# A hybrid decoder block on one core: three weight tiles rounded into other rooms, 512-column products in the compressed branch, one gate for both attention groups, keys copied out by ACT

## The chip, the cores and the metric

The kernel runs on one core of one Trainium2 chip. The metric is the device time of one execution in microseconds (us). The time before is the median of three runs. Profiles and traces come from one execution recorded by the hardware profiler, whose own time is told beside its span.

## The reference

One decoder layer over 512 tokens of width 1024, all in float32. The input is normalised, projected by `w_in`, and goes through two mixers whose results are gated and merged:

```python
h = rms_norm(x, norm_pre)
proj = h @ w_in
(q_n, k_c, v_c, k_s, v_s, k_w, v_w, g_n, z_n,
 q_r, k_r, v_r, z_r, m_a, m_b) = jnp.split(proj, split_points(), axis=-1)
...
def compress_blocks(kv, pe, w1, w2):
    ...
    flat = blocks.transpose(0, 2, 1, 3).reshape(n_cmp, G, CMP_LEN * dh)
    return jax.nn.gelu(flat @ w1) @ w2
...
y_a = (o_a * jax.nn.silu(z_n)) @ w_nsa_o
...
q_r = apply_rotary(q_r.reshape(B, S, RET_HEADS, RET_QK_DIM), ret_ang)
k_r = apply_rotary(k_r.reshape(B, S, RET_HEADS, RET_QK_DIM), ret_ang) * (RET_QK_DIM ** -0.5)
o_b = jax.vmap(retention_sequence)(q_r, k_r, v_r.reshape(B, S, RET_HEADS, RET_V_DIM))
y_b = (o_b * jax.nn.silu(z_r)) @ w_ret_o
merged = jax.nn.sigmoid(m_a) * y_a + jax.nn.sigmoid(m_b) * y_b
x = x + rms_norm(merged @ w_out, norm_post)
```

Mixer A is sparse attention with 8 heads of 64 in two key/value groups and three branches (compressed, selected, sliding). In the compressed branch 32 tokens of keys or values are flattened and go through a small network: `flat @ w1` has 2048 inputs and 256 hidden units, once for keys and once for values. Mixer B is retention with 4 heads in chunks of 128 tokens.

## The kernel before

**Split products.** Every float32 operand of a matmul is kept as a rounded high part and a low part (the remainder, rounded). A product is three matmuls: high by high, high by low and low by high. A weight tile of 128x512 therefore goes three ways. A load brings 128x1024 from memory into `raw` (4 slots, issued on SP, L373). ACT (L200) or DVE (L208) copies half of it rounded into `whi`. DVE subtracts (L212, `wlo<-raw,whi`); this is called a split below. The pairs `whi`, `wlo` are rings of NW = 9 places; a place is free again when the last product with its tile is done. A raw slot is free when both its halves are split. The 8 weight tiles of block C (280 columns) have rooms of their own (`WC`). The tiles are numbered by the order in which PE uses them; tiles 24 to 39 are those of the compressed branch.

**Stages of PE.** The main row of the program, in order: A (x by the first weights, 4 tiles at once), C (280 columns of small projections, 4 token tiles t), Q (the attention queries, t from 3 down to 0), the hidden layer of the compressed branch for keys and for values (`hidden(0)`, `hidden(1)`), Z, MA, ZR, then the retention queries and keys, values and state, MB, the output products of both mixers, and the last product. Z and the later blocks have 512 columns. The attention itself (scores, softmax, products with values, in units of a token tile t and a group g) is interleaved behind Q. Some products are done by sums of quarters, whose operands (`hs`, `wmT`, `wqT`) are added up on DVE or by POOL's DMAs, written to memory and loaded again.

**What sets the order.** A static list scheduler (`Order`) writes all instructions while the program is built. It models the clocks of the engines; each piece of work is a generator that yields the time or the event it needs, and the scheduler issues the piece with the best priority that its model holds ready. Each engine then runs its rows in exactly this order. The weight rounding has the priority `rank(p)`: 0 (first) when its tile is due within a window of the model's time, 4 otherwise; for the tiles 24 to 39 the window is 4000 ns. A change of a cost or a condition can thus move rows on every engine.

**What the change touches.** `PHL` is a ring of three rooms of 1024 columns for attention's probabilities, split into both parts, and `PC` is one room for the compressed branch; all lie in `arena_r`. `qT[t]` holds the split and transposed queries. `hidden(i)` multiplies the flattened blocks `Xs[i]`: per weight tile and half of it two matmuls of 256 columns, moving `whi` and `wlo`, summed in the same PSUM half. `compress` goes on with that sum. `att_sum` gathers one unit (t, g), gates it (DVE, `szn`), and writes the result over the gate. `tail_qk` without `base` takes the keys of retention out of PSUM with their row scale `rs` and applies the rotary tables in four `SCALAR_TENSOR_TENSOR` operations of 256 columns per token tile. `ga_split` splits the gated attention for the output product. PSUM banks come from the rings ACC, PS, PT and PO with two banks each.

## Time and profile before

| | us |
|---|---|
| median of 3 runs | 511.99 (511.87 to 512.14) |
| profiled execution | 512.8 |
| its span | 511.0 |
| mean granted TensorE clock | 0.996 |

The profile names groups of instructions by line, engine, operation and tile: `L233 PE MATMUL bank<-whi,hTh` is a matmul of line 233 that writes a PSUM bank from the tiles whi and hTh. PE is TensorE's matmul, PEld its weight load, DVE VectorE, ACT ScalarE, POOL GpSimd, SP the engine that issues DMAs. In timeline rows the first number is the start in us from the span's start, the second the length of the row (several alike instructions may be one row, with their count), and the bracket holds the idle time before it and what ended it. In rows of groups the numbers behind the bar are busy us in all, mean ns of one, and idle us before them. The ends of matmuls are modelled and overlap the next start, so paces are read from starts.

### The profile page before, as it was taken

Reading aid. Unit: us, or ns where it says so; the run is one execution under the profiler, and the core shown is the slowest. Engines: PE = TensorE matmul, PEld = TensorE weight load, DVE = VectorE, ACT = ScalarE, POOL = GpSimd, SP = SyncE. Lnnn points to the kernel's source line nnn. Section 1 sums busy time; section 2 is a strip of 40 time slices with the busy share of each in tenths; the row PEclk is TensorE's granted clock in tenths of the full one; section 3 lists DMA queues with packets and bytes.
Section 4 is the critical chain, followed back from the end, with each engine's and each line's share of the span. In section 5 each row is a group of like instructions: output and inputs, shape, how many; then the busy total and the mean of one; then the engine's idle time right before and its main releaser. Section 6 shows DMA issues by size and latency. Waiting matters only on the chain.

```text
span 511.0 us, 7894 instructions
## 1 busy us (share of the span) xinstructions
PE 501.7 (98%) x2700; PEld 429.6 (84%) x2700; DVE 424.4 (83%) x984; ACT 312.7 (61%) x675; POOL 50.2 (10%) x82
## 2 busy tenths in 40 slices
PE   8999999999999999999999999999999999999994
PEld 7898789888888888888888878888888999888884
DVE  6799699979979799898689899785757769969887
ACT  5788589755777769755585667554614445427541
POOL 2100100002000000101212010311010000000011
PEclk9999999999999999999999999999999999999998
DMA  8996667967921733958389989376875996314826
GB/s 309 378 337 216 177 150 227 345 144 160 252 41 50 223 60 107 325 126 226 79 249 290 315 270 304 61 208 123 279 177 152 322 387 249 123 41 147 275 50 148
DMA packets 34248, 103.47 MB, mean 202 GB/s; under 512 B 3600, under 2 KB 8080, under 8 KB 34192
## 3 DMA queue, kind: packets, MB, share of 16 engines
q1 hardware_dynamic: 29312, 85.41, 47.1%
q0 software_dynamic: 4752, 17.30, 20.0%
q8 instruction: 21, 0.34, 0.3%
q10 hardware_dynamic: 144, 0.26, 0.2%
q14 instruction: 19, 0.16, 0.1%
HBM read 98.76 MB, written 34.08 MB: 260 GB/s over the span
## 4 chain that ended last, share of the span: by engine, by line
PE 80%; DVE 11%; DMA 7%; issue 1%; ACT 1%; SPq 0%; DVEq 0%; ACTq 0%
PE bank L233 74%; DMA raw<-in_stream_dram 7%; PE bank L237 6%; DVE wlo L212 3%; DVE arena_f L212 3%; DVE arena_r L212 2%; DVE nat L212 1%; DVE arena_f L225 1%; DVE arena_f L688 0%; ACT whi L200 0%; ACT arena_r L200 0%; SPq L605 0%; DVE whi L208 0%; DVE st L1362 0%; DVE hTl L225 0%
## 5 line engine op out<-in xcount | busy, mean ns | idle before, releaser
L212 DVE TENSOR_TENSOR wlo<-raw,whi 128x512 fp32r<-128x512 f32 x196 | 127.7, 685 | 9.1 <-ACT whi L200 8.5
L200 ACT ACTIVATE whi<-raw 128x512 fp32r<-128x512 f32 x175 | 103.1, 624 | 46.4 <-PE bank L233 23.3
L233 PE MATMUL bank<-whi,hTh 128*128 128x512 f32 x248 | 96.1, 403 | 0.0
L233 PE MATMUL bank<-whi,hTl 128*128 128x512 f32 x248 | 93.3, 392 | 0.3 <-DVE hTl L225 0.3
L233 PE MATMUL bank<-wlo,hTh 128*128 128x512 f32 x248 | 93.0, 391 | 0.0
L233 PE MATMUL bank<-arena_r 128*128 128x256 f32 (+2 forms) x328 | 69.3, 337 | 0.0
L233 PE MATMUL bank<-hTh,whi 128*128 128x512 f32 (+1 forms) x192 | 66.2, 345 | 0.0
L233 PE MATMUL bank<-arena_r,whi 128*128 128x512 f32 (+1 forms) x224 | 64.9, 374 | 0.0
L233 PE MATMUL bank<-hTh,wlo 128*128 128x512 f32 (+1 forms) x192 | 64.8, 338 | 0.0
L233 PE MATMUL bank<-hTl,whi 128*128 128x512 f32 (+1 forms) x192 | 64.7, 337 | 0.0
L200 ACT ACTIVATE arena_r<-bank 128x512 fp32r<-128x512 f32 (+2 forms) x76 | 42.5, 569 | 30.7 <-PE bank L237 28.3
L233 PEld LDWEIGHTS bank<-whi,hTl 128*128 128x128 f32 x248 | 46.4, 188 | 11.2 <-DVE hTl L225 1.0
L233 PEld LDWEIGHTS bank<-arena_r 128*128 128x128 f32 x328 | 50.3, 189 | 5.7
L233 PEld LDWEIGHTS bank<-whi,hTh 128*128 128x128 f32 x248 | 46.6, 188 | 8.7 <-ACT hTh L200 0.2
L233 PEld LDWEIGHTS bank<-wlo,hTh 128*128 128x128 f32 x248 | 46.7, 188 | 8.4
L212 DVE TENSOR_TENSOR arena_r<-bank,arena_r 128x512 fp32r<-128x512 f32 (+2 forms) x68 | 43.9, 654 | 11.2 <-ACT arena_r L200 10.8
L200 ACT ACTIVATE arena_f<-arena_f,stat 128x128 f32<-128x128 f32 (+3 forms) x88 | 47.5, 552 | 7.2 <-DVE stat L212 4.1
L233 PEld LDWEIGHTS bank<-arena_r,whi 128*128 128x128 f32 x224 | 41.0, 188 | 7.4
L233 PE MATMUL bank<-whi,arena_r 128*128 128x512 f32 (+1 forms) x152 | 44.5, 359 | 0.0
L233 PE MATMUL bank<-arena_r,wlo 128*128 128x512 f32 (+1 forms) x112 | 41.9, 374 | 0.0
L233 PEld LDWEIGHTS bank<-hTh,wlo 128*128 128x128 f32 x192 | 36.4, 190 | 4.1
L233 PEld LDWEIGHTS bank<-hTh,whi 128*128 128x128 f32 x192 | 36.5, 190 | 3.0
(160 smaller groups left out, 773.2 us busy)
## 6 DMA issues: line engine op xcount, KB each, us to landing
raw<-in_stream_dram SPq DMA_DIRECT2D x73, 512.0 KB, 4.8
arena_f<-in_xT_dram SPq DMA_DIRECT2D x16, 256.0 KB, 6.0
wqT<-in_stream_dram POOLq DMA_DIRECT2D x8, 512.0 KB, 5.5
wmT<-in_stream_dram POOLq DMA_DIRECT2D x8, 512.0 KB, 8.0
raw<-wqT SPq DMA_DIRECT2D x8, 512.0 KB, 5.3
woT<-in_stream_dram POOLq DMA_DIRECT2D x8, 512.0 KB, 5.6
raw<-wmT SPq DMA_DIRECT2D x8, 512.0 KB, 5.1
raw<-woT SPq DMA_DIRECT2D x8, 512.0 KB, 3.4
```

The costliest lines, as they stand in the source:

```text
L200: S.activation(o, i, func, **kw)
L212: (V if e == "dve" else G).tensor_tensor(o, a, b, op=op)
L225: V.scalar_tensor_tensor(o, a, s, b, op0=op0, op1=op1)
L233: T.matmul(ps, a, b, start=start, stop=stop)
L237: T.transpose(ps, a, idn)
```

## The change

Four things are changed, and the scheduler's order with them.

1. The tiles 25, 26 and 27 (the second to fourth of `hidden(0)`) no longer take a place of the ring. They have rooms in `arena_r` that stand empty until later: those of `PHL` and `PC` (tiles 25 and 26) and that of `qT[0]` (tile 27). `PHL` begins with one room and `PC` with none; both get theirs when tile 26 is used, and `qT[0]` waits for tile 27 (flag "away"). The window of `rank` becomes 4500 for tiles 24 to 31 and the common one for 32 to 39.
2. `whi` and `wlo` become one tile `whl` with both parts side by side. `hidden` issues one matmul of 512 columns (256 of the high part, 256 of the low) instead of two of 256, so the two sums stand in two halves of a bank, and `compress` adds them.
3. The gate of the attention is applied once per token tile for both groups (`att_gate`, 128 partitions) instead of once per group (64 partitions). `ga_split` waits for it by flags of its own.
4. `tail_qk` without `base` has ACT copy the keys with their scale from PSUM; the rotary tables are then applied from this copy, with two multiplications of 256 columns and one of 512.

```diff
@@ -267,8 +267,8 @@
     Xs = [at(44 + 8 * i, 2048, FR).rearrange("p (l s c) -> p l s c", l=16, s=2) for i in range(2)]
-    PHL = Ring([at(o, 1024, FR) for o in (60, 64, 40)])
-    PC = Ring([at(68, 512, FR)])
+    PHL = Ring([at(o, 1024, FR) for o in (40,)])
+    PC = Ring([])
     qk = [at(44 + 4 * t, 1024, FR).rearrange("p (s c) -> p s c", s=2) for t in range(NT)]
@@ -355,9 +355,11 @@
+    away = {25: 62, 26: 66, 27: 0}
+
     def in_ring(p):
-        return min(p, KD) + max(p - 2 * KD, 0)
+        return min(p, KD) + max(p - 2 * KD, 0) - sum(q < p for q in away)
     hook = {}
@@ -388,7 +390,7 @@
                 p = 2 * i + k
-                own = KD <= p < 2 * KD
+                own = KD <= p < 2 * KD or p in away
                 yield lambda: own or in_ring(p) < in_ring(len(done)) + NW
@@ -398,16 +400,23 @@
                 src = raws[i][0][:, k * m:(k + 1) * m]
-                if own:
+                if p in away:
+                    both = at(away[p], 1024, FR).rearrange("p (s c) -> p s c", s=2)
+                    hi, lo = both[:, 0, :], both[:, 1, :]
+                    pairs_of[p] = both
+                elif own:
                     hi, lo = WC[p - KD]
                 else:
-                    hi = wp.tile([P, 512], FR, name="whi", tag="whi", bufs=NW)
-                    lo = wp.tile([P, 512], FR, name="wlo", tag="wlo", bufs=NW)
+                    both = wp.tile([P, 2, 512], FR, name="whl", tag="whl", bufs=NW)
+                    hi, lo = both[:, 0, :], both[:, 1, :]
+                    pairs_of[p] = both
                 vh, vl = hi[:, :m], lo[:, :m]
...
                 yield
+
+    pairs_of = {}
@@ -528,7 +537,7 @@
             b = now_in[0]
-            return 0 if b is None or b.until(p) <= (4000.0 if 24 <= p < 40 else SOON) else 4
+            return 0 if b is None or b.until(p) <= (4500.0 if 24 <= p < 32 else SOON) else 4
         return fn
@@ -805,13 +814,23 @@
             yield blk.ready(c)
-            hi, lo, r = blk.views(c)
+            r = blk.views(c)[2]
             for l in range(2):
                 st = Xs[i][:, 2 * c + l].rearrange("p s c -> p (s c)")
-                mm(ph[:, 0:256], st, hi[:, l * 256:(l + 1) * 256], c + l == 0, False, r)
-                e = mm(ph[:, 0:256], st, lo[:, l * 256:(l + 1) * 256], False, c + l == 8)
+                e = mm(ph, st, pairs_of[blk.base + c][:, :, l * 256:(l + 1) * 256], c + l == 0, c + l == 8, r,
+                       0.4418 * 512 + 1)
                 yield
             used_up(e)
+            p = blk.base + c
+            if p in away:
+                if away[p] == 66:
+                    PHL.put(at(60, 1024, FR), e)
+                    PHL.put(at(64, 1024, FR), e)
+                    PC.put(at(68, 512, FR), e)
+                elif away[p] == 40:
+                    PHL.put(at(40, 1024, FR), e)
+                elif away[p] == 0:
+                    od.flags.add("away")
         od.spawn(compress(i, ph, e), 1)
@@ -819,7 +838,9 @@
         u = at(35 + 0.5 * i, 128).rearrange("p (k c) -> p k c", k=2)
-        e = act(hs, ph[:, 0:256], r=e)
+        e = act(hs, ph[:, 256:512], r=e)
+        yield e, "dve"
+        e = tt(hs, ph[:, 0:256], hs, OP.add, e)
         ACC.put(ph, e)
@@ -877,6 +898,8 @@
         qv = qn.rearrange("p (h c) -> p h c", h=8)
+        if t == 0:
+            yield od.need("away")
         e = act(qs[:, :, 0, :], qv, r=e)
@@ -1082,18 +1105,20 @@
         m, o = slice(g * 64, g * 64 + 64), slice(64 - g * 64, 128 - g * 64)
-        low = yield from NAT.get()
+        if g:
+            yield lambda: t in lows
+        low = lows[t][0] if g else (yield from NAT.get())
+        if not g:
+            lows[t] = (low, [])
         yield a["e"], "act"
...
         PO.put(po, e)
-        yield e, "pool"
-        gv = szn[m, :, t * P:(t + 1) * P]
-        e = tt(gv, low[m].rearrange("p (j c) -> p j c", j=4), gv, OP.mult, e)
-        NAT.put(low, e)
-        zr_[0] = max(zr_[0], e)
+        lows[t][1].append(e)
         od.flags.add(f"att{t}{g}")
+        if len(lows[t][1]) == 2:
+            od.spawn(att_gate(t), 1)
         if t == 2 and all(f"att{i}{j}" in od.flags for i in (2, 3) for j in range(2)):
@@ -1106,6 +1131,16 @@
+    def att_gate(t):
+        low, e = lows[t][0], max(lows[t][1])
+        yield e, "dve"
+        gv = szn[:, :, t * P:(t + 1) * P]
+        e = tt(gv, low.rearrange("p (j c) -> p j c", j=4), gv, OP.mult, e)
+        NAT.put(low, e)
+        zr_[0] = max(zr_[0], e)
+        od.flags.add(f"gz{t}")
+
+    lows = {}
     ATT = tuple(f"att{t}{g}" for t in range(NT) for g in range(2))
@@ -1144,7 +1179,6 @@
         v2 = t2.rearrange("p (a r c) -> p a r c", a=4, r=2)
-        pv = ps.rearrange("p (a r c) -> p a r c", a=4, r=2)
         if base:
@@ -1153,19 +1187,15 @@
             e = act(t1, t1, r=e, scale=rs(t))
-            r = max(e, rtr[4 * hp + t])
-            yield r, "dve"
-            for i in range(2):
-                tt(v2[:, :, i, :], v1[:, :, 1 - i, :], tv[:, 1], OP.mult, r)
-            e = tt(v1, v1, tv[:, 0].unsqueeze(2).broadcast_to([P, 4, 2, 64]), OP.mult, r)
         else:
-            yield max(e, rtr[4 * hp + t]), "dve"
-            for i in range(2):
-                e = stt(v1[:, :, i, :], pv[:, :, i, :], rs(t), tv[:, 0], OP.mult, OP.mult, e)
-            yield e, "dve"
-            stt(v2[:, :, 0, :], pv[:, :, 1, :], rs(t), tv[:, 1], OP.mult, OP.mult, e)
-            e = stt(v2[:, :, 1, :], pv[:, :, 0, :], rs(t), tv[:, 1], OP.mult, OP.mult, e)
+            yield e, "act"
+            e = act(t1, ps, r=e, scale=rs(t))
             ACC.put(ps, e)
+        r = max(e, rtr[4 * hp + t])
+        yield r, "dve"
+        for i in range(2):
+            tt(v2[:, :, i, :], v1[:, :, 1 - i, :], tv[:, 1], OP.mult, r)
+        e = tt(v1, v1, tv[:, 0].unsqueeze(2).broadcast_to([P, 4, 2, 64]), OP.mult, r)
         if hp == 0 and t < NT - 1:
@@ -1461,7 +1491,7 @@
     def ga_split():
-        yield od.need(*RETA)
+        yield od.need(*RETA, *[f"gz{t}" for t in range(NT)])
         for j in range(4):
@@ -1864,7 +1894,8 @@
-    hi, lo = (wp.tile([P, 512], FR, name=n, tag=n, bufs=NW) for n in ("whi", "wlo"))
+    both = wp.tile([P, 2, 512], FR, name="whl", tag="whl", bufs=NW)
+    hi, lo = both[:, 0, :], both[:, 1, :]
     r = raws[0][1] - 600
```

In all, PE has 64 matmuls of 256 columns less and 32 of 512 more (2656 instead of 2688, with as many weight loads). DVE has 16 `SCALAR_TENSOR_TENSOR` less, 8 multiplications of 256 and 4 of 512 columns more for the keys, 4 gates of 128x512 in place of 8 of 64x512, and 2 additions of 256 columns. ACT has 4 copies of 512 columns more. The rows of all engines are the same up to about 38 us of the trace before; from 38 to 249 us they are shuffled; PE's are the same again from 249 to 312 us and from about 333 us on.

Three places show how rows move. The first is PE in block Q, where the first transposes of a finished query tile stand (`identr,arena_r`, x4). `bank_84` and `bank_83` are the banks of the tiles of Q. Before, and of the change:

```order
L237 MATMUL bank_87<-ident,arena_f 128x128 x2
L233 MATMUL bank_84<-whi,hTh 128x512
L233 MATMUL bank_84<-wlo,hTh 128x512
L233 MATMUL bank_84<-whi,hTl 128x512
L233 MATMUL bank_84<-whi,hTh 128x512
L233 MATMUL bank_84<-wlo,hTh 128x512
L233 MATMUL bank_84<-whi,hTl 128x512
L237 MATMUL bank_88<-identr,arena_r 128x128 x4
L233 MATMUL bank_84<-whi,hTh 128x512
```

```order
L233 MATMUL bank_83<-whl,hTh 128x512 x2
L233 MATMUL bank_83<-whl,hTl 128x512
L237 MATMUL bank_87<-ident,arena_f 128x128 x2
L233 MATMUL bank_83<-whl,hTh 128x512 x2
L233 MATMUL bank_83<-whl,hTl 128x512
L233 MATMUL bank_83<-whl,hTh 128x512 x2
L233 MATMUL bank_83<-whl,hTl 128x512
L237 MATMUL bank_88<-identr,arena_r 128x128 x4
L233 MATMUL bank_83<-whl,hTh 128x512 x2
```

Before, the transposes stand in Q's second tile, behind 45 of its 96 products; of the change in the third tile, behind 57.

The second is DVE in the same stretch. `wlo<-raw,whi` (of the change `whl<-raw,whl`) is a split of a ring tile, `arena_r<-raw,arena_r` the split of a tile in one of the rooms; `arena_f<-bank,cst` makes the compressed branch's input. Before, and of the change:

```order
L212 TENSOR_TENSOR wlo<-raw,whi 128x512 x3
L212 TENSOR_TENSOR arena_f<-bank_88,cst 64x2x16x8 x4
L212 TENSOR_TENSOR arena_r<-bank_87,arena_r 128x2x128
L212 TENSOR_TENSOR wlo<-raw,whi 128x512
L688 COPY arena_f<-nat_107 128x256
L212 TENSOR_TENSOR arena_r<-nat_107,arena_r 128x64 x2
L212 TENSOR_TENSOR arena_r<-arena_f,arena_r 128x16x64 x2
L212 TENSOR_TENSOR arena_r<-bank_87,arena_r 128x2x128
```

```order
L212 TENSOR_TENSOR whl<-raw,whl 128x512
L212 TENSOR_TENSOR arena_f<-bank_87,cst 64x2x16x8 x4
L212 TENSOR_TENSOR whl<-raw,whl 128x512
L212 TENSOR_TENSOR arena_f<-bank_88,cst 64x2x16x8 x4
L212 TENSOR_TENSOR arena_r<-raw,arena_r 128x512 x3
L212 TENSOR_TENSOR arena_r<-arena_f,arena_r 128x16x64
L212 TENSOR_TENSOR arena_r<-bank_88,arena_r 128x2x128
L212 TENSOR_TENSOR arena_r<-arena_f,arena_r 128x16x64
```

The three splits of the tiles 25 to 27 stand ahead of the splits of the branch's input (`arena_r<-arena_f,arena_r`), and those come ahead of the split of the transposed keys.

The third is ACT and DVE around 277 to 295 us, in the retention stage. `whi<-raw` is the rounding of a weight tile (the numbers tell the loads apart: `raw_2935` before and `raw_2813` of the change are the same load), `arena_f<-bank7,nm,rv` normalises retention's output, `arena_r<-arena_r` rounds a sum of quarters `hs` that was loaded again, and `arena_r<-bank5` takes a transpose out of PSUM. ACT before, and of the change:

```order
L200 ACTIVATE whi_2928<-raw_2872 128x512
L200 ACTIVATE whi_2937<-raw_2872 128x512
L200 ACTIVATE whi_2988<-raw_2893 128x512
L200 ACTIVATE whi_2991<-raw_2893 128x512
L200 ACTIVATE arena_f_81<-bank7_90,nm_2972,rv_2964 128x256 x2
L200 ACTIVATE whi_3011<-raw_2935 128x512
L200 ACTIVATE whi_3017<-raw_2935 128x512
L200 ACTIVATE whi_3032<-raw_2957 128x512
L200 ACTIVATE whi_3035<-raw_2957 128x512
L200 ACTIVATE arena_r_82<-arena_r_82 128x512 x2
L200 ACTIVATE arena_r_82<-bank5_88 128x4x128
```

```order
L200 ACTIVATE whl_2815<-raw_2757 128x512
L200 ACTIVATE whl_2833<-raw_2757 128x512
L200 ACTIVATE whl_2835<-raw_2778 128x512
L200 ACTIVATE whl_2837<-raw_2778 128x512
L200 ACTIVATE whl_2877<-raw_2813 128x512
L200 ACTIVATE arena_f_81<-bank7_90,nm_2855,rv_2847 128x256 x2
L200 ACTIVATE whl_2890<-raw_2813 128x512
L200 ACTIVATE whl_2895<-raw_2840 128x512
L200 ACTIVATE arena_r_82<-arena_r_82 128x512 x2
L200 ACTIVATE whl_2911<-raw_2840 128x512
L200 ACTIVATE arena_r_82<-bank5_88 128x4x128
```

The first half of that load is rounded ahead of the pair `arena_f<-bank7,nm,rv`, and `arena_r<-bank5` stands behind one rounding more. DVE behind it (`maskp` and `arena_f` take sums of products, and the keys `nat` follow some ten rows later), before, and of the change:

```order
L212 TENSOR_TENSOR arena_r<-arena_r 128x512 x2
L212 TENSOR_TENSOR arena_r<-bank_88,arena_r 128x4x128
L212 TENSOR_TENSOR arena_f<-bank_83,arena_f 128x512
L212 TENSOR_TENSOR wlo<-raw,whi 128x512 x2
L212 TENSOR_TENSOR maskp<-bank_86,maskp 128x512
L212 TENSOR_TENSOR wlo<-raw,whi 128x512 x4
L212 TENSOR_TENSOR arena_f<-bank_84,arena_f 128x512
L212 TENSOR_TENSOR arena_r<-arena_r 128x512 x2
L208 CAST whi<-raw 128x512
L212 TENSOR_TENSOR wlo<-raw,whi 128x512
L225 SCALAR_TENSOR_TENSOR arena_f<-nat_110,arena_f 128x512
L212 TENSOR_TENSOR arena_f<-bank_83,arena_f 128x512
```

```order
L212 TENSOR_TENSOR arena_r<-arena_r 128x512 x2
L212 TENSOR_TENSOR arena_r<-bank_88,arena_r 128x4x128
L212 TENSOR_TENSOR whl<-raw,whl 128x512 x2
L212 TENSOR_TENSOR arena_f<-bank_85,arena_f 128x512
L212 TENSOR_TENSOR whl<-raw,whl 128x512 x2
L212 TENSOR_TENSOR maskp<-bank_84,maskp 128x512
L212 TENSOR_TENSOR whl<-raw,whl 128x512 x3
L212 TENSOR_TENSOR arena_r<-arena_r 128x512 x2
L212 TENSOR_TENSOR arena_f<-bank_83,arena_f 128x512
L208 CAST whl<-raw 128x512
L212 TENSOR_TENSOR whl<-raw,whl 128x512 x2
L212 TENSOR_TENSOR arena_f<-bank_85,arena_f 128x512
```

Between the same first and last rows DVE has nine splits instead of seven; the next rows up to `nat` hold three splits in both.

## The prediction

> **What bounds the kernel now.** The page comes first: whose work fills the span, and which engine carries the chain that ended last.
>
> ```profile
> span 511.0 us, 7894 instructions
> PE 501.7 (98%) x2700; PEld 429.6 (84%) x2700; DVE 424.4 (83%) x984; ACT 312.7 (61%) x675; POOL 50.2 (10%) x82
> PE 80%; DVE 11%; DMA 7%; issue 1%; ACT 1%; SPq 0%; DVEq 0%; ACTq 0%
> ```
>
> PE is busy 98% of the span. A microsecond saved on another engine is therefore worth something only where PE waits for it, and a microsecond of PE's own work is worth itself. The second view is the table of windows, cut where the order of the work differs between the kernels (its columns: window, its length, busy time of PE, PEld, DVE, ACT, POOL, granted clock, DMA share, GB/s).
>
> ```profile
> 28.00:58.00 30.00, 29.54 (x189) 25.50 (x189) 26.55 (x94) 22.11 (x61) 2.53 (x5) 1.00 0.75 253
> 58.00:92.00 34.00, 34.00 (x209) 29.57 (x209) 31.12 (x78) 29.61 (x65) 1.92 (x2) 1.00 0.71 190
> 92.00:205.00 113.00, 113.00 (x590) 95.82 (x589) 98.47 (x272) 79.99 (x195) 8.67 (x9) 1.00 0.56 152
> 205.00:262.00 57.00, 57.00 (x303) 47.99 (x302) 46.99 (x120) 36.37 (x86) 8.25 (x12) 1.00 0.68 192
> 262.00:306.00 44.00, 43.34 (x213) 35.91 (x212) 40.46 (x79) 28.36 (x53) 5.37 (x9) 1.00 0.96 289
> ```
>
> From 58 to 262 us PE is busy all the time at the full granted clock. It loses time in the first window (30.00 − 29.54 = 0.46 us) and in the last (0.66 us), where the DMA share is 0.96. The third view, PE's waits, names who is late there.
>
> ```profile
> PE bank L237 <- DVE nat L212: 0.5, 1, 0.5
> PE bank L237 <- DVE arena_f L688: 0.3, 1, 0.3
> PE bank L237 <- DVE arena_r L212: 0.2, 1, 0.2
> ```
>
> PE waits for single results of DVE: a copy of `arena_f` (0.3, at 30 us, where both orders are the same), the first split Q tile (0.2), and the retention keys `nat` at 304 us (0.5). The time beside these waits is PE's pace. So the change has three ways to act: by PE's own work, at the first transposes of Q, and at the transposes of `nat`.
>
> **Part 1, the products of the compressed branch.** 64 matmuls of 256 columns become 32 of 512, with the same products.
>
> ```profile
> 77.43 0.28 PE L233 MATMUL bank<-wlo,arena_r 128*128 128x256 f32 x1
> ...
> 80.07 0.28 PE L233 MATMUL bank<-wlo,arena_r 128*128 128x256 f32 x1
> ...
> 23.93 1.07 PE L233 MATMUL bank<-wlo,hTh 128*128 128x512 f32 x4
> 24.84 1.07 PE L233 MATMUL bank<-whi,hTh 128*128 128x512 f32 x4
> ```
>
> The ends of matmuls overlap in the timeline, so the pace is read from starts. From 77.43 to 80.07 there are 22 steps, (80.07 − 77.43)/22 = 0.120 us for a 256-column product with its weight load. Four 512-column ones take 24.84 − 23.93 = 0.91 us, 0.2275 each. The change is worth 32 × 0.2275 − 64 × 0.120 = 7.28 − 7.68 = **−0.40 us**. It lies on PE in a window without waits, so nothing hides it.
>
> ```profile
> L233 PEld LDWEIGHTS bank<-arena_r 128*128 128x128 f32 x328 | 50.3, 189 | 5.7
> ```
>
> The 32 weight loads that go take 0.189 us each, longer than the whole 0.120 us step, so most of a load lies under other matmuls here. The Trainium skill ("TensorE: Matmul & The Clock Gate", section "The mechanism") states that a load overlaps matmuls in flight only where the row groups differ. These all use 128 rows, and the trace disagrees with that rule; by it the loads would count in full (last rival). The same page (section "Wait — 56ns, not 53.3ns?") gives N/2.4 + 2.5 ns as the step; by that estimate the part saves 64 × 0.109 − 32 × 0.216 = 0.08 us, and the sum below would be 0.3 higher. The paces of the trace are used.
>
> **Part 2, three tiles rounded ahead (38 to 58 us).** Tiles 25 to 27 no longer wait for ring places. ACT's three casts and DVE's three splits move ahead, and Q's tiles run further before the first Q transposes.
>
> ```profile
> 55.27 0.40 PE L233 MATMUL bank<-whi,hTl 128*128 128x512 f32 x1
> 55.84 0.54 PE L237 MATMUL bank<-identr,arena_r 128*128 128x128 f32 x4 [0.17 <-DVE arena_r L212]
> ...
> 45.02 1.89 DVE L212 TENSOR_TENSOR wlo<-raw,whi 128x512 fp32r<-128x512 f32 x3
> 46.83 1.74 DVE L212 TENSOR_TENSOR arena_f<-bank,cst 64x256 f32<-64x256 f32 x4
> ```
>
> PE's start at 55.84 comes 0.57 after the one before it instead of 0.23: a stall of 0.34 (the row books 0.17, since the modelled end overlaps). In the new order 57 products of Q stand ahead of these transposes, not 45: PE arrives 12 × 0.2275 = 2.7 us later. DVE has the three splits more ahead of it, 1.8 us (45.02 to 46.83). 1.8 is under 2.7, so the stall goes: **−0.34**. Bounds: the window shows no other wait in reordered work, so no more can go; the 1.8 could be uncovered at the transposes of the compressed keys, which stand earlier: from −0.34 to +1.8. I take −0.34, the end with a row.
>
> ```profile
> 35.29 0.49 ACT L200 ACTIVATE nat<-bank,rs 128x280 f32<-128x280 f32 x1 [0.85 <-PE bank L233]
> ...
> L200 ACT ACTIVATE whi<-raw 128x512 fp32r<-128x512 f32 x175 | 103.1, 624 | 46.4 <-PE bank L233 23.3 <-DMA raw<-in_stream_dram 13.6 <-DMA raw<-wmT 6.5
> ```
>
> On ACT the three casts (3 × 0.62 = 1.9) stand ahead of this copy. ACT idles 0.85 before it, so the copy comes about 1.0 us later. It frees a PSUM bank that only the fourth tile of this stage takes again, so I cost it at 0; without that cover it would cost up to 1.0. The two loads are issued where they were, so SP and POOL gain nothing and lose nothing here.
>
> **Part 3, attention gate, retention keys, halves added.** The operations with their mean times:
>
> ```profile
> L225 DVE SCALAR_TENSOR_TENSOR nat<-bank,rs,arena_f 128x256 f32<-128x256 f32 x16 | 6.8, 473 | 0.4 <-DMA arena_f<-in_rope_r_dram 0.3
> L212 DVE TENSOR_TENSOR nat<-nat,arena_f 128x256 f32<-128x256 f32 x12 | 4.7, 419 | 0.0
> L212 DVE TENSOR_TENSOR nat<-nat,arena_f 128x512 f32<-128x512 f32 x4 | 2.8, 692 | 0.1
> L212 DVE TENSOR_TENSOR arena_f<-nat,arena_f 64x512 f32<-64x512 f32 x8 | 5.5, 684 | 0.2
> L200 ACT ACTIVATE nat<-bank,rs 128x512 f32<-128x512 f32 x8 | 5.3, 687 | 0.5 <-PE bank L233 0.4
> ```
>
> DVE loses 16 × 0.473 = 7.6 of the keys and 8 × 0.684 = 5.5 of the gate. It gains 8 × 0.419 + 4 × 0.692 = 6.1 for the keys, 4 × 0.69 = 2.8 for the gate and 2 × 0.42 = 0.8 for the halves: −3.4 in all. ACT gains 4 × 0.69 = 2.7. All of it lies before 262 us, where PE never waits, so I take **0**. The cover is PE's own queue of products. Were it gone, a key tile would hold its bank 0.4 us longer (0.69 + 2 × 0.42 + 0.69 = 2.2 on two engines in turn, against 4 × 0.473 = 1.9 on one): up to 4 × 0.4 = +1.6, and below nothing no wait of PE is there to be removed. The gate's later flags (both groups) are waited for by the splits of `gah`, which no PE wait of the trace names.
>
> **Part 4, what the new order does at 262 to 306 us.** DVE's work freed earlier does not help here; the order on ACT and DVE differs and costs. ACT and DVE before:
>
> ```profile
> 277.61 1.02 ACT L200 ACTIVATE arena_f<-bank,nm,rv 128x256 f32<-128x256 f32 x2 [3.07 <-POOL nm L212]
> 279.61 2.43 ACT L200 ACTIVATE whi<-raw 128x512 fp32r<-128x512 f32 x4 [0.98 <-DMA raw<-in_stream_dram]
> 283.05 1.15 ACT L200 ACTIVATE arena_r<-arena_r 128x512 fp32r<-128x512 f32 x2 [1.00 <-DMA arena_r<-hs]
> ...
> 278.67 0.69 DVE L212 TENSOR_TENSOR arena_f<-arena_f 128x512 f32<-128x512 f32 x1
> 283.71 1.29 DVE L212 TENSOR_TENSOR arena_r<-arena_r 128x512 fp32r<-128x512 f32 x2 [1.28 <-ACT arena_r L200]
> ...
> 280.34 0.60 PE L237 MATMUL bank<-ident,arena_f 128*128 128x128 f32 x4
> ```
>
> First place: in the new order one cast from the load that landed at 279.5 stands ahead of the pair `arena_f<-bank,nm,rv`. ACT runs its rows in order, so the pair starts at 279.61 + 0.61 = 280.2 instead of 277.61, 2.6 later; so do DVE's product (278.67 + 0.69 = 279.36) and PE's transposes, which have 280.34 − 279.36 = 0.98 in hand. PE stalls 2.6 − 0.98 = 1.6 us. The Trainium skill (the same page, section "Architectural detail: the array is 16× 32×32, not 1× 128×128") calls ACT's and DVE's queues strictly first in, first out, which speaks against this edit; the trace's rows agree, and only an ACT that took the pair past the waiting cast would remove this stall.
>
> Second place, which decides the end:
>
> ```profile
> 301.00 0.39 PE L233 MATMUL bank<-whi,arena_r 128*128 128x512 f32 x1
> 301.50 0.63 PE L237 MATMUL bank<-ident,nat 128*128 128x128 f32 x4
> ...
> 303.84 0.40 PE L233 MATMUL bank<-whi,hTl 128*128 128x512 f32 x1
> 304.78 0.63 PE L237 MATMUL bank<-ident,nat 128*128 128x128 f32 x4 [0.54 <-DVE nat L212]
> ```
>
> PE stalls here 0.50 − 0.23 = 0.27 and 0.94 − 0.23 = 0.71, together 0.98, for DVE, which is busy nearly without a gap from 283.71. Between the two `arena_r<-arena_r` splits and `nat`, DVE has two weight splits more in the new order: 2 × 0.60 = 1.2. One ACT cast more ahead of `arena_r<-bank` makes DVE wait some 0.35 (284.93 to about 285.3), and 0.13 of waiting for a load goes. So `nat` comes 1.2 + 0.35 − 0.13 = 1.42 later, and with it the transposes at 304.78: PE's 1.6 at the first place is not added, it is taken up in this wait. Term: **+1.42**. Bounds: 0 if the `hs` load lands 1.28 earlier against PE (DVE's idle time at 283.71), about +3 if PE's 1.6 were added in full.
>
> **The sum.** −0.40 − 0.34 + 0 + 1.42 = +0.68. The profiled execution took 512.8 us, the median of the runs is 511.99, 0.8 lower; so 513.5 as profiled, 512.7 for the median.
>
> **Rivals.**
> - *Slower: the loads do not come earlier.* My sum lets everything at 262 to 306 us move 0.74 forward with PE. At a DMA share of 0.96 the landing of the `hs` load (ACT at 283.05) may be set by the queues' backlog. Then the 0.74 is eaten there, DVE starts its row at 283.71 as before, and the price is +1.42: 513.4; with each microsecond of later landing one more. It decides from 0.4 us of lost advance. For it: the share, and both waits of ACT on DMA. Against: DVE's chain from 263 to 273 us, which releases these loads, follows PE.
> - *Slower still: the three splits are uncovered in the first window*: +1.8 for −0.34, so −0.40 + 1.8 + 1.42 = +2.8, 514.8.
> - *Faster: the waits of both windows shrink.* Loads land over 2.4 us earlier against PE, so the 1.42 finds cover and the 0.98 goes too: −0.40 − 0.34 − 0.98 = −1.72, 510.3. For it: 1.28 of idle DVE and 1.00 of idle ACT before 283.71. Against: the 0.96.
> - *Covered: nothing is late at 304 us that was not before*: −0.40 − 0.34, or −0.40 if the early rounding does not reach Q's transposes: 511.3 to 511.6.
> - *The loads of weights count in full*: 32 × 0.189 = −6.0, 506 to 507. The page named for the row groups would have it; the 0.120 steps exclude it but for a chance of 1%.
>
> **How the numbers follow.** A measurement of this kernel tells about 0.2%, 1.02 us: faster is below 511.0, slower above 513.0. My forecast of 512.7 has 0.36, covered 0.09: same 0.45. Loads that do not come earlier 0.25, uncovered splits 0.06: slower 0.31. Faster 0.23, with full loads 0.01: 0.24. The range runs from 510.2, the faster rival's number rounded down, to 514.0, half a microsecond of later landing beyond the slower one; it leaves out the full loads, the splits uncovered and the tails of both, under 0.2.
>
> **What would show it.** The compressed products should start 0.2275 apart, 16 for each half of the branch. The identr transposes of the first Q tile should start 0.23 after the product ahead of them. ACT should show a cast ending in the wait for a load and the nm,rv pair right behind it, about 2.6 us after POOL's `nm`, and PE a wait of over 1 us for DVE's `arena_f` near 280 us. The waits for `nat` near 305 should remain. Between 58 and 262 us PE should stay without waits. If PE runs through 280 us without a wait, part 4's first place is wrong; if the `nat` waits fall below 0.5 us together, its second; if PE waits anywhere in 92 to 262 us, part 3.

## The result, and the profile after

| | before | changed |
|---|---|---|
| median, 20 runs each | 511.94 us | 515.01 us |
| range | 511.5 to 513.13 | 511.89 to 517.56 |
| ratio | | 1.0055, 95% interval 1.0042 to 1.0068 |
| profiled execution (its span) | 512.8 (511.0) | 517.56 (515.8) |

The change makes the kernel slower by 3.1 us, more than the 0.7 that was forecast and outside the range. Its runs also spread over 5.7 us, those of before over 1.6. The execution that was profiled is the slowest of the twenty, so its waits are likely among the largest.

The waits of PE in the changed kernel (total us, times, longest):

```profile
PE bank L237 <- DVE stat L229: 2.2, 1, 2.2
...
PE bank L237 <- DVE arena_f L212: 0.3, 1, 0.3
...
PE bank L233 <- DVE whl L212: 0.3, 1, 0.3
PE bank L237 <- DVE nat L212: 0.2, 1, 0.2
```

The 0.5 for `nat` has shrunk and the 0.2 for `arena_r` from DVE is no longer listed. The wait for `arena_f` from L212, which the forecast put at over 1 us near 280 us, is 0.3 long. A wait of 2.2 us is new, and the forecast does not know it. The windows (window, length, busy time of PE, PEld, DVE, ACT, POOL, granted clock, DMA share, GB/s) say where it is:

```profile
205.00:262.00 57.00, 54.47 (x282) 45.30 (x281) 42.22 (x111) 36.44 (x90) 7.53 (x11) 0.97 0.59 156
...
227.00:230.00 3.00, 0.76 (x5) 0.38 (x4) 2.97 (x8) 0.64 (x3) 0.00 (x0) 1.00 0.26 79
230.00:234.00 4.00, 4.00 (x13) 3.13 (x12) 4.00 (x12) 3.98 (x10) 0.00 (x0) 0.57 0.46 155
234.00:238.00 4.00, 4.00 (x23) 3.34 (x22) 3.96 (x9) 3.35 (x7) 0.31 (x1) 1.00 0.76 235
```

The window 205 to 262 us, in which PE had no idle time before, now has 2.5 us of it. Behind the wait the granted clock is 0.57 for about 4 us: PE starts 13 matmuls there, against 23 in the next 4 us. The clock's drop costs nearly as much again as the wait (4 × (1 − 0.57) = 1.7 us).

PE's timeline at that place (start, length, then the row):

```profile
227.02 0.39 PE L233 MATMUL bank<-whl,hTl 128*128 128x512 f32 x1
229.65 0.63 PE L237 MATMUL bank<-ident,nat 128*128 128x128 f32 x4 [2.24 <-DVE stat L229]
```

DVE's timeline of the changed kernel, ahead of that:

```profile
219.78 1.48 DVE L212 TENSOR_TENSOR nat<-nat,arena_f 128x256 f32<-128x256 f32 x3
221.18 0.68 DVE L212 TENSOR_TENSOR arena_f<-nat,arena_f 128x512 f32<-128x512 f32 x1
...
224.12 0.08 DVE L1001 DVE_READ_ACCUMULATOR2_ANT stat<- 128x1 f32 x1
226.75 1.49 DVE L212 TENSOR_TENSOR nat<-nat,arena_f 128x256 f32<-128x256 f32 x3 [2.54 <-ACT whl L200]
```

And the table's load, in the view of its line of the changed kernel between 221 and 222 us (time of the issue in ns, its start in us, and the landing):

```profile
L1173 SPq DMA_DIRECT2D arena_f<-in_rope_r_dram x1: 333/333/333, 221.3 to 221.3; - x1
...
DMA to landing us min/median/max: 5.3/5.3/5.3
```

The row at 226.75 applies the rotary table to a key tile. Its idle time is booked on an ACT rounding (`whl`) that it does not read. What it reads is the table, and that has one room: the table of this tile was issued at 221.3, when DVE had used the last one (219.78 to 221.18), and landed 5.3 us later, at 226.6. DVE had 3 us of other work to put between (its rows from 221.18 to 224.2). Everything behind that row on DVE waits too, among it the keys that PE transposes next. In the kernel before, SP's and DVE's timelines show the same piece so:

```profile
222.92 0.33 SPq L1138 DMA_DIRECT2D arena_f<-in_rope_r_dram  x1
...
226.67 0.39 SPq L1102 DMA_DIRECT2D arena_f<-in_dmask_dram  x1
```

```profile
224.68 0.90 DVE L208 CAST whi<-raw 128x512 fp32r<-128x512 f32 x2
225.50 1.29 DVE L212 TENSOR_TENSOR wlo<-raw,whi 128x512 fp32r<-128x512 f32 x2
...
228.25 0.88 DVE L225 SCALAR_TENSOR_TENSOR nat<-bank,rs,arena_f 128x256 f32<-128x256 f32 x2
```

The table issued at 222.92 is used at 228.25, 5.3 us later, and DVE has weight casts and splits in that time. This load landed after 2.7 us, so it was covered.

### The profile page after: what moved, and what is told of

The parts are those of the page before. It is cut to its first block, busy times and chain, and to the rows that moved or that the text cites. A ratio compares the mean times of both kernels' runs of the same rounds, so it can differ in the third digit from the quotient of the medians.

```text
span 515.8 us, 7806 instructions
## 1 busy us (share of the span) xinstructions
PE 503.6 (98%) x2668; PEld 428.8 (83%) x2668; DVE 419.8 (81%) x979; ACT 315.9 (61%) x680; POOL 50.2 (10%) x82
## 4 chain that ended last, share of the span: by engine, by line
PE 81%; DMA 7%; DVE 7%; issue 1%; ACT 1%; SPq 1%; DVEq 0%; ACTq 0%
PE bank L233 75%; PE bank L237 6%; DMA raw<-in_stream_dram 5%; DVE whl L212 2%; DMA arena_f<-in_dmask_dram 2%; DVE nat L212 1%; DVE arena_f L212 1%; DVE arena_r L212 1%; DMA raw<-wqT 1%; DVE arena_f L225 1%; DVE arena_f L1001 1%; ACT arena_f L200 0%; ACT whl L200 0%; SPq L614 0%; ACT arena_r L200 0%
## 5 line engine op out<-in xcount | busy, mean ns | idle before, releaser
L233 PE MATMUL bank<-whl,hTh 128*128 128x512 f32 x496 | 153.9, 399 | 0.0
L200 ACT ACTIVATE whl<-raw 128x512 fp32r<-128x512 f32 x171 | 101.8, 625 | 54.0 <-PE bank L233 28.6
L212 DVE TENSOR_TENSOR whl<-raw,whl 128x512 fp32r<-128x512 f32 x193 | 125.2, 683 | 10.7 <-ACT whl L200 10.6
L233 PEld LDWEIGHTS bank<-whl,hTh 128*128 128x128 f32 x496 | 90.9, 190 | 17.7 <-ACT hTh L200 0.5
L233 PE MATMUL bank<-hTh,whl 128*128 128x512 f32 (+1 forms) x384 | 102.6, 342 | 0.0
L233 PE MATMUL bank<-whl,hTl 128*128 128x512 f32 x248 | 93.9, 394 | 0.0
L233 PEld LDWEIGHTS bank<-hTh,whl 128*128 128x128 f32 x384 | 66.2, 190 | 6.9
L233 PE MATMUL bank<-arena_r,whl 128*128 128x512 f32 (+1 forms) x336 | 71.6, 374 | 0.0
L233 PEld LDWEIGHTS bank<-arena_r,whl 128*128 128x128 f32 x336 | 59.8, 188 | 11.2
L233 PE MATMUL bank<-hTl,whl 128*128 128x512 f32 (+1 forms) x192 | 64.7, 337 | 0.0
L212 DVE TENSOR_TENSOR arena_r<-bank,arena_r 128x512 fp32r<-128x512 f32 (+2 forms) x68 | 43.6, 652 | 16.3 <-ACT arena_r L200 16.1
```

Of the source, the lines that this page charges most:

```text
L200: S.activation(o, i, func, **kw)
L212: (V if e == "dve" else G).tensor_tensor(o, a, b, op=op)
L233: T.matmul(ps, a, b, start=start, stop=stop)
```

## The experiments

Some of the kernels hold the scheduler's model as it is and change only what is issued, so that the other rows keep their places; others let it plan anew. This difference turned out to matter most.

**The table, and the kernel again.**

```diff
+    rtab2 = at(24, 512)
-        return rtab if i < 4 else zt[0][i - 4]
+        return (rtab, rtab2)[i % 2] if i < 4 else zt[0][i - 4]
...
-        DMA.dma_start(rtab_of(i), rope_r[i // 4, i % 4 * P:(i % 4 + 1) * P, :])
+        for j in {0: (0, 1), 1: (2,), 2: (3,), 3: ()}.get(i, (i,)):
+            DMA.dma_start(rtab_of(j), rope_r[j // 4, j % 4 * P:(j % 4 + 1) * P, :])
```

> The changed kernel with the rotary tables of the keys in two rooms by turns, so that each table of tiles 1 to 3 is loaded one tile earlier; every row of PE, DVE, ACT and POOL stays as in the changed kernel. Theory 1 (the table's load, released only by the last use of the one room, is what DVE waits for at 224 to 227 us, PE waits 2.2 us behind it, and the granted clock drops to 0.57 for 4 us after that): the wait for stat and the clock's drop are gone, PE is busy 57.0 of 57 us in the window 205 to 262, the median falls from 515.0 to between 512.0 and 513.5, and the runs lie within 2 us of each other. Theory 2 (the wait is one of many, and what it frees is taken again at the next one): the median stays above 514.3.

Measured: 513.55 (512.61 to 515.77), against 515.38 for the changed kernel on the same chip. DVE's row now follows without idle time (DVE's timeline of this kernel):

```profile
224.04 1.48 DVE L212 TENSOR_TENSOR nat<-nat,arena_f 128x256 f32<-128x256 f32 x3
```

Its window from 205 to 262 us:

```profile
205.00:262.00 57.00, 57.00 (x308) 48.32 (x308) 46.20 (x119) 41.12 (x99) 8.46 (x12) 1.00 0.65 177
```

In this profiled execution (512.64, near the fastest of its ten) the wait and the clock's drop are gone and PE is busy 57.00 of 57.00; 1.8 us of the median (515.38 − 513.55) have gone: the table's load is shown as the largest single cause. The median is a little above the 513.5 expected and the spread is 3.2 us against the 2 expected, so it is not the only one.

> The changed kernel once more. If the landing of the table's load sets its time from run to run (theory 1), the times spread again over 3 us or more, and in the new profile the wait of PE near 229 us is larger or smaller along with its time: a profiled execution near 513 shows under 0.5 us of it, one near 517 over 2. If the spread comes from elsewhere (theory 2), the wait is about 2 us whatever the time.

Measured: 515.38 (513.29 to 517.67). In the profiled execution, of 514.33, the same wait is 0.9 us in the list of waits:

```profile
PE bank L237 <- DVE stat L229: 0.9, 1, 0.9
```

and the window behind it has the clock at 1.00:

```profile
228.00:232.00 4.00, 4.00 (x21) 3.31 (x20) 4.00 (x12) 3.98 (x10) 0.00 (x0) 1.00 0.49 174
```

DVE's row stands 1.18 us in this execution, and here the wait is booked on the table itself (DVE's timeline):

```profile
224.91 1.49 DVE L212 TENSOR_TENSOR nat<-nat,arena_f 128x256 f32<-128x256 f32 x3 [1.18 <-DMA arena_f<-in_rope_r_dram]
```

The load was issued at 220.8 and took 4.0 us to land, against 5.3 in the other execution. The same program so waits 2.24 us in one execution and 0.88 in another, and only the longer wait has the clock's drop behind it. Both together, 1.36 + 1.7 = 3.1 us, account for the distance of the two executions (517.56 − 514.33 = 3.2 us).

**The decay mask.** It is loaded when attention ends, which the changed order puts later: 238.19 instead of 226.67 (SP's row of before, above). The chain of the changed kernel runs through its landing (start, us, what):

```profile
238.19 8.79 DMA arena_f<-in_dmask_dram
...
247.07 0.44 DVE arena_f L212
```

Behind it PE stands 0.3 us. The mask is given the table's old room and is loaded with the last key tile:

```diff
-    dm = at(20, 512).rearrange("p (h c) -> p h c", h=4)
+    dm = at(28, 512).rearrange("p (h c) -> p h c", h=4)
...
-            DMA.dma_start(dm, dmask.rearrange("h p c -> p h c"))
...
+        if i == 3:
+            DMA.dma_start(dm, dmask.rearrange("h p c -> p h c"))
```

> The first kernel of this set with the decay mask in the freed table room, so that its load is issued with the last key tile and not at the end of attention; the rows of PE, DVE, ACT and POOL stay as in the changed kernel. If the mask's load (8.8 us from issue to landing, DVE idle 1.1 for it near 247 us) costs PE the 0.8 us that its starts lose between 244 and 252 us, the median is 0.4 to 0.9 us under that of the first kernel; if that stall is covered by what follows, within 0.3 of it.

Measured: 512.99 (1.0016, interval 1.0003 to 1.0030), 0.56 under the kernel with the table's rooms alone, as expected if the mask costs; but that kernel's own interval, 1.0005 to 1.0040 around 1.0022, covers this one. Called "rooms and mask" below, it was run again:

> The kernel of the run with rooms and mask once more, for its distance to the kernel before and for a second profile. With the two waits of 205 to 262 us gone, theory 1 leaves the waits at 76 to 92 us (1.5 us in its first profile, 0.3 before) and at 276 to 284 us (0.7): 512.6 to 513.4, ratio 1.001 to 1.003. If the distance seen so far (1.0016) was chance, it comes out within 0.9995 to 1.0005.

Measured: 513.23, 1.0024 (1.0013 to 1.0035), as theory 1 expected, and as far above the kernel before as the table's rooms alone are. In the profile of the kernel with the table's rooms alone the mask is still loaded at the end of attention, and the row that uses it follows without idle time (DVE's timeline):

```profile
241.39 0.42 DVE L212 TENSOR_TENSOR arena_f<-bank,arena_f 128x256 f32<-128x256 f32 x1
241.86 0.43 DVE L212 TENSOR_TENSOR arena_f<-arena_f 128x256 f32<-128x256 f32 x1
```

So the mask was late in the profiled execution of the changed kernel, but it is not shown that it costs anything in the median. Of the 3.1 us, 1.8 are shown to be the table's; 1.0 to 1.2 us are left in "rooms and mask".

**The key tail by itself.**

```diff
-            for i in range(2):
-                e = stt(v1[:, :, i, :], pv[:, :, i, :], rs(t), tv[:, 0], OP.mult, OP.mult, e)
-            ...
+            yield e, "act"
+            e = act(t1, ps, r=e, scale=rs(t))
             ACC.put(ps, e)
```

> The kernel before with part 3's key tail alone: ACT copies the keys out, DVE applies the tables from the copy. Theory 1a (the loss is in the key tail itself, which leaves too little work between a table's last use and the next one): slower than 511.9 by 1.5 us or more. Theory 1b (the loss is in the order that all parts together make; in this kernel's order some 12, 6 and 5 us of DVE work lie between the uses, as before): between 511.4 and 512.6, no wait of PE for DVE over 0.5 us between 205 and 262 us.

Measured: 511.99, ratio 1.0003 (0.9988 to 1.0018). Planned anew around the new tail, the kernel is as fast as before, as theory 1b expected. Then the same edit put into the rows of before, the model unaware of it:

> The kernel before with the key tail alone (ACT copies, DVE applies the tables from the copy), the order of all other rows held as before: ACT's copy stands where DVE's first operation stood. My term: 0, with a bound of +1.6 where the copy and DVE in turn hold a key tile longer. Theory 1 (only the cover between the uses of a table matters; here it stays some 12, 6 and 5 us): 0.9990 to 1.0010. Rival (the tail itself delays DVE's row, which waits for ACT's copy 0.7 us each time): above 1.002.

Measured: 1.0043 (1.0031 to 1.0056), so the rival holds for a tail put into rows that make no allowance for it, and theory 1 alone is too narrow. ACT's timeline of this kernel, and DVE's:

```profile
227.19 0.59 ACT L200 ACTIVATE nat<-bank 64x512 f32<-64x512 f32 x1
227.81 2.48 ACT L200 ACTIVATE arena_r<-arena_r 128x512 fp32r<-128x512 f32 x4
230.20 0.58 ACT L200 ACTIVATE arena_r<-bank 128x512 fp32r<-128x512 f32 x1
230.68 0.68 ACT L1162 ACTIVATE nat<-bank,rs 128x512 f32<-128x512 f32 x1
```

```profile
223.31 0.76 DVE L1165 TENSOR_TENSOR nat<-nat,arena_f 128x256 f32<-128x256 f32 x2 [1.83 <-ACT nat L1162]
...
231.39 0.76 DVE L1165 TENSOR_TENSOR nat<-nat,arena_f 128x256 f32<-128x256 f32 x2 [1.41 <-ACT nat L1162]
```

DVE stands 1.83 and 1.41 us for ACT's copy, which ACT reaches, in the second case, only behind four roundings of `arena_r` and two copies out of PSUM. PE waits behind it three times between 226 and 236 us, for 0.17, 0.35 and 0.54 us, the last time here (PE's timeline):

```profile
235.41 0.66 PE L237 MATMUL bank<-ident,nat 128*128 128x128 f32 x4 [0.54 <-DVE nat L212]
```

This loss belongs to the place of the copy in the old rows: in the changed kernel DVE waits for the copy once, 0.27 us at 205 us.

**The products by themselves**, again in the rows of before:

```diff
-                mm(ph[:, 0:256], st, hi[:, l * 256:(l + 1) * 256], c + l == 0, False, r)
-                e = mm(ph[:, 0:256], st, lo[:, l * 256:(l + 1) * 256], False, c + l == 8)
+                T.matmul(ph, st, pairs_of[blk.base + c][:, :, l * 256:(l + 1) * 256], start=c + l == 0, stop=c + l == 8)
+                od.pe(0.4418 * 256 + 1, r)
+                e = od.pe(0.4418 * 256 + 1)
...
+        V.tensor_tensor(hs, ph[:, 0:256], hs, op=OP.add)
```

> The kernel before with the 512-column products alone (the pair tile, 32 matmuls for 64, and the two additions of halves), and with the order of all other rows held as before: the scheduler still counts two products of 256 columns. My term: -0.40, so 0.9992 of the kernel before (511.5 against 511.9). If PE, which comes earlier to tiles that are not split yet, waits for it between 84 and 96 us: 1.000, with 0.4 us more of waiting there in the profile.

Measured: 1.0033 (1.0021 to 1.0044), slower by 1.7 us and worse than both expectations. The addition of the halves is late, in DVE's timeline of this kernel, and PE's behind it waits:

```profile
92.55 0.42 DVE L843 TENSOR_TENSOR arena_f<-bank,arena_f 128x256 f32<-128x256 f32 x1 [0.96 <-ACT arena_f L200]
92.89 0.68 DVE L212 TENSOR_TENSOR arena_r<-bank,arena_r 128x512 fp32r<-128x512 f32 x1
```

```profile
93.63 0.66 PE L233 MATMUL bank<-arena_f 128*128 128x64 f32 x4 [1.12 <-DVE arena_r L212]
```

DVE waits 0.96 us for ACT's copy of the other half and adds for 0.34; a split behind it is late by that, and PE waits 1.12. In the changed kernel neither addition (80.26 and 90.90 us) has idle time of DVE before it, so this loss, too, belongs to the place in the old rows.

> Both of the kernels above together: the kernel before with the products and the key tail, in the order of before. The sum of my terms: -0.40, 511.5, under both kernels of the case. If the terms do not add (the products' gain is given back): 0.9995 to 1.0010.

Measured: 1.0064 (1.0051 to 1.0076), a little under the sum of the two losses (0.33% and 0.43%) and above both expectations. No version was found that beats the kernel before.

**Parts of the change, planned anew.** Three kernels let the scheduler plan: one is told that table loads take longer, one has the old gate, one has neither gate nor key tail changed.

```diff
-        rtr[i] = od.dma(P * 2048, r)
+        rtr[i] = od.dma(P * 2048, r) + 2500.0
```

The old gate, against the changed kernel:

```diff
-        low = lows[t][0] if g else (yield from NAT.get())
+        low = yield from NAT.get()
...
+        gv = szn[m, :, t * P:(t + 1) * P]
+        e = tt(gv, low[m].rearrange("p (j c) -> p j c", j=4), gv, OP.mult, e)
+        NAT.put(low, e)
...
-        if len(lows[t][1]) == 2:
-            od.spawn(att_gate(t), 1)
```

The third has this and, besides, the key tail of before (the edit of the key tail above, the other way round).

> The changed kernel with one number changed: the scheduler counts 2.5 us more for each load of a rotary table, so that it puts other work ahead of a key tile that waits for its table. The instructions are those of the changed kernel, in another order: some 10, 8 and 7 us of DVE work now lie between a table's last use and the next use (9, 3 and 8 before this edit). Theory 1 (the cover over the table's load decides): no wait of PE over 0.5 us and no drop of the clock between 205 and 262 us, median 511.5 to 513.0. Theory 2 (the changed parts cost by themselves): above 514.

> The changed kernel with the gate per group as before (part 3a undone). Its order leaves some 10, 2.5 and 7 us of DVE work between the uses of the tables. Theory 1 (cover decides, whatever the gate): as slow as the changed kernel, 514 to 516, with a wait of PE of 1 us or more near 229 us. Rival (the common gate, which holds a buffer for both groups and ends attention later, is the cause): 511.5 to 512.5.

> The changed kernel without parts 3a and 3b (gate and key tail as before): only the 512-column products of the compressed branch and the three tiles rounded ahead. My terms for these two were -0.40 and -0.34: 511.2 if they stand. If the microsecond that PE is ahead at 76 us is lost again between 76 and 92 us, where DVE and ACT are busy without a gap (both are at 4.00 of 4 us from 84 to 88), the median is 511.7 to 512.4.

Measured: 522.13, 523.26 and 521.56, against 511.94 for the kernel before on the same chip: 9.6 to 11.3 us more, which none of the expectations had. In the first the table's wait is gone as meant, but PE waits 0.8 us at 244 us and longer further on (PE's timeline, then the window behind):

```profile
274.90 0.65 PE L237 MATMUL bank<-ident,arena_f 128*128 128x128 f32 x4 [2.69 <-DVE arena_f L212]
```

```profile
276.00:280.00 4.00, 4.00 (x19) 3.68 (x18) 3.86 (x9) 0.82 (x2) 0.44 (x1) 0.57 0.43 109
```

In the kernel with the old gate the table's wait is there (DVE's timeline, this time booked on the load), and a longer one beside it (PE's timeline):

```profile
227.33 1.49 DVE L212 TENSOR_TENSOR nat<-nat,arena_f 128x256 f32<-128x256 f32 x3 [2.48 <-DMA arena_f<-in_rope_r_dram]
```

```profile
230.82 0.94 PE L237 MATMUL bank<-ident,nat 128*128 128x128 f32 x4 [2.00 <-DVE nat L212]
...
279.72 1.11 PE L237 MATMUL bank<-ident,arena_f 128*128 128x128 f32 x4 [3.10 <-DVE arena_f L212]
```

In the third, with neither gate nor key tail changed, PE waits for a key tile as well, without a drop of the clock (PE's timeline):

```profile
231.80 0.73 PE L233 MATMUL bank<-whl,hTh 128*128 128x512 f32 x2 [1.68 <-DVE nat L225]
```

These runs cannot price a part: each draws another order of some 2,650 matmuls, and orders that look alike in work differ by 10 us. Which of the edits led the scheduler to leave so little work between two tables in the changed kernel therefore stays open.

**The cast ahead of the pair.** The first place of part 4, undone alone in the rows of "rooms and mask": ACT's rounding of the late tile is issued behind the pair `arena_f<-bank,nm,rv`.

```diff
+                if p == 96:
+                    late.append((vh, src))
+                    e = od.op("act", act_ns(vh, src), r)
...
+        while late and (hp, t) == (0, 3):
+            S.activation(*late.pop(), AF.Copy)
         PS.put(po, e)
```

> The kernel of the run with rooms and mask, with one ACT instruction moved: the rounding of the tile whose load lands last stands behind the pair that normalises retention's output, as before the change; every other row stays. My first place of part 4 (a stall at 280 us): that run lost 0.69 us between 276 and 280 us by PE's starts; this should fall under 0.2. By my second place (DVE two splits later, which takes up the first) the end moves by less than 0.4: median within 0.4 of 512.99. If the stall stands by itself, the median falls by 0.5 or more.

Measured: 513.55, ratio 1.0025 (1.0015 to 1.0035), against 1.0016 and 1.0024 of the kernel without this edit. It did not fall, so the stall does not stand by itself; 513.55 is 0.56 over 512.99, outside the 0.4 expected, but the ratios do not differ beyond their intervals. The wait at 280 us goes, and others stand at 304 us and later (PE's timeline):

```profile
279.95 0.60 PE L237 MATMUL bank<-ident,arena_f 128*128 128x128 f32 x4
303.96 0.63 PE L237 MATMUL bank<-ident,nat 128*128 128x128 f32 x4 [0.44 <-DVE nat L212]
314.99 0.63 PE L237 MATMUL bank<-ident,nat 128*128 128x128 f32 x4 [0.24 <-DVE nat L212]
```

**More profiles.** 

> The kernel before, for a second profile beside the first. If its waits at 302 to 305 us (1.0 us in the first profile) are what puts that execution 0.8 over the median, an execution near 512.0 shows under 0.4 us of them; if the start up to 32 us varies instead (1.6 us of waits in the first profile), that part is shorter.

> As the run ahead of it: a third profile of the kernel before. Between 76 and 92 us it should lose 0.3 us by PE's starts, as in the first.

> The kernel with rooms and mask, for a third profile. If the rest of the loss lies at 76 to 92 us and 276 to 284 us, it loses 1.2 to 1.5 and 0.7 us there in each profile, against 0.3 and 0.1 in the kernel before, and 0.4 less on the products.

> As the run ahead of it: a fourth profile of the kernel with rooms and mask. An execution of 513.5 or more should show where it differs from one of 512.5.

Measured: profiled executions of 512.57 and 512.82 (before), 513.39 and 512.13 (rooms and mask). Of the waits at 302 to 305 us the second profile of the kernel before has 0.4 us, counted by starts, against 1.0 in the first, and its execution is 0.2 us shorter, so they explain only a part of the 0.8. The third has its 0.3 us at 76 to 92 us, as expected. No execution of 513.5 or more was caught; the two of 513.39 and 512.13 differ by 0.6 us at 76 to 92 us and by 0.4 at 260 to 320. The table sums, by stage, what PE's steps from start to start have over the pace of their kind (0.227 us for 512 columns, 0.120 for 256, about 0.11 for a transpose), in us:

| stage | before, three profiles | rooms and mask, four profiles |
|---|---|---|
| 32 to 76 | 1.22, 1.22, 1.24 | 0.52, 0.58, 0.51, 0.60 |
| 76 to 92 | 0.27, 0.27, 0.28 | 1.53, 1.22, 1.77, 1.20 |
| 92 to 260 | 0.75, 1.28, 0.94 | 0.59, 0.62, 0.60, 0.61 |
| 260 to 320 | 1.25, 0.57, 1.39 | 1.44, 1.37, 1.60, 1.24 |

Means of the differences: −0.67, +1.16, −0.38, +0.34, and −0.40 for the products' pace: together +0.05. The sums hang on the paces taken: with the median step of each kind of matmul as its pace, the four differences are −0.89, +1.05, −0.31 and +0.35, so they are good to some 0.2 us. The profiles so agree with each other: their executions took 512.73 (before) and 512.71 (rooms and mask) in the mean. The distance of 1.0 to 1.2 us between the medians, however, is not in them. The profiled executions of before lie some 0.7 over its median, those of the other kernel some 0.4 under. Where the rest of the distance is in executions without a profile stays open.

## Why the prediction was wrong

- **Part 3 failed**, at "All of it lies before 262 us, where PE never waits, so I take 0". By the prediction's own sign (a wait of PE anywhere in 92 to 262 us) it is the part that is wrong. In the profiled execution PE stands idle for 2.5 us between 205 and 262 us, and the clock's drop behind the wait adds 1.7. That PE did not wait was a property of the old order, not a reserve in DVE: before, 5.3 us lay between a table's issue and its use, for a landing of 2.7; the new order leaves 3 us of work for a landing of 5.3. A second room for the table takes back 1.8 of the 3.1 us. The row of `L225` shown in Part 3 names this very load as what ended DVE's idle time. The last key tile already waited for its table in the kernel before (DVE's timeline of its first profile):

```profile
236.30 1.66 DVE L225 SCALAR_TENSOR_TENSOR nat<-bank,rs,arena_f 128x256 f32<-128x256 f32 x4 [0.27 <-DMA arena_f<-in_rope_r_dram]
```

  The table landed 5.1 us after its issue there, and PE did not wait behind it. In the second profile of the same kernel it took 5.7 us, DVE stood 0.85 us and PE 0.50 (PE's timeline):

```profile
240.22 0.66 PE L237 MATMUL bank<-ident,nat 128*128 128x128 f32 x4 [0.50 <-DVE nat L212]
```

  In the third it took 4.5 us and neither waited. So "never waits" was true of the one profile that the prediction had, not of the kernel. The bound of +1.6 was built on another mechanism, a bank held longer, and that is misread: by the diff the bank goes back right behind ACT's copy (0.69 us), earlier than behind the four operations of before (1.9 us); and 2.2 − 1.9 is 0.3, not 0.4. That the tail alone cost 2.2 us in the old rows does not confirm the bound, since there DVE waits for ACT; planned anew it cost nothing. The mask's later load was not in the forecast either; its price is not shown.

- **Part 1** has the right pace and the wrong sum. In the changed kernel four such products take 78.64 − 77.72 = 0.92 us, 0.23 each (PE's timeline):

```profile
77.72 1.07 PE L233 MATMUL bank<-whl,arena_r 128*128 128x512 f32 x4
78.64 0.46 PE L237 MATMUL bank<-identr,arena_r 128*128 128x128 f32 x4
...
80.16 0.54 PE L237 MATMUL bank<-identr,arena_r 128*128 128x128 f32 x4 [0.29 <-ACT arena_r L200]
...
84.69 1.33 PE L233 MATMUL bank<-whl,arena_r 128*128 128x512 f32 x4 [0.26 <-DVE whl L212]
```

  and the window around them, before and in the changed kernel:

```profile
76.00:92.00 16.00, 16.00 (x114) 14.62 (x113) 15.82 (x35) 14.74 (x33) 0.00 (x0) 1.00 0.75 239
76.00:92.00 16.00, 15.44 (x79) 11.85 (x78) 15.73 (x35) 12.86 (x27) 0.00 (x0) 1.00 0.78 257
```

  But "nothing hides it" was wrong. Between 76 and 92 us DVE was busy 15.82 of 16 us before and is busy 15.73 now, so it has nothing to give. PE, which comes earlier, waits there for a copy of ACT (0.29 us) and for a split of DVE (0.26): in "rooms and mask" the stage loses 1.2 us more by starts than before, and parts 1 and 2 together (−0.40 − 0.67 + 1.16) come out at +0.1. The additions of the halves, costed inside DVE's balance, lie in this full stretch.
- **Part 2** was right and undersized: no wait for DVE at the first Q transposes, −0.67 instead of −0.34 from 32 to 76 us. It is given back right behind.
- **Part 4** named a wait at both places and oversized the sum: +0.34 between 260 and 320 us instead of +1.42. The first place lost 0.6 to 0.8 us in three of four profiles (0.05 in the fourth), less than 1.6, since the load landed earlier (the pair started at 278.72 in "rooms and mask", not at 280.2). The second place does take up the first: with the cast moved back, the wait moved on to 304 to 316 us and the median did not fall. The `hs` load, on which the bound rested, was cast from 280.86 us on instead of 283.05, which can cover most of the two splits; that it does was not tested (ACT's timeline of "rooms and mask"):

```profile
278.72 1.00 ACT L200 ACTIVATE arena_f<-bank,nm,rv 128x256 f32<-128x256 f32 x2
279.62 1.14 ACT L200 ACTIVATE whl<-raw 128x512 fp32r<-128x512 f32 x2
280.86 1.15 ACT L200 ACTIVATE arena_r<-arena_r 128x512 fp32r<-128x512 f32 x2
```

- Of the **rivals**, the slower one named the right class, a load that is late, but another load, 50 us too late in the program and at too low a price, since neither the spread of landings nor the clock's drop was in it.
- **What stays open**: the 1.0 to 1.2 us between the medians of "rooms and mask" and of the kernel before, and which edit made the order leave the table uncovered.

## What to carry to other kernels

When a static order is planned anew, look at every load whose room is freed by the last use of what it replaces: the work that the new order leaves on the using engine between that use and the next must cover the load's longest landing, not its modelled one; a second room costs no engine time. In the table of stages above, the time that PE saved was lost again in a stretch in which DVE, which feeds it, was full; so a term is checked stage by stage against the feeder. Undoing parts with a fresh plan compares orders, not edits. Holding the order and changing only the rows in question is better, but it also prices the place at which the new row happens to stand: the key tail cost 2.2 us in the old rows and nothing when it was planned for. The clean test here was the one that moved a load and no row of an engine.

## What was not expected of the hardware

A short stop of PE cost nearly twice its length: behind the wait of 2.24 us the granted clock was 0.57 from 230 to 234 us, worth 1.7 us. It dropped in the same way behind a wait of 2.7 us (0.57 from 276 to 280 us, table loads told longer) and, with the old gate, behind one of 2.0 us (0.53 from 230.8 to 234.3) and around one of 3.1 us that ended at 279.7 (0.51 from 278.6 to 289.1, a stretch with another wait of 1.5 us in it). Behind waits of 0.9, 1.1 and 1.7 us (in the changed kernel again, the products in the old rows, and the products and rooms) it stayed at 1.00. So the longest wait without a drop was 1.7 us and the shortest with one 2.0 us; these seven waits do not show that the length alone decides. The Trainium skill ("TensorE: Matmul & The Clock Gate", section "Why this matters for your kernels") asks for no idle gaps over about 3 us between bursts of matmuls; here a shorter one was enough, and the measurement decides.

The eight table loads of the kernel before, 256 KB each, took 2.7 to 9.4 us from issue to landing within one execution, and one and the same load of the changed kernel took 5.3 us in one execution and 4.0 in another, and PE's wait behind it was 2.24 and 0.88 us.
